# Gathered rows scaled and shifted while they are turned, instead of before they are stored

## The chip, the cores and the metric

The kernel runs on one core of one Trainium2 chip. Its time is the device time of one execution in microseconds (us), given as the median of several executions. The profile is of one further execution of the same program; its rows are in us from the start of its span, and durations in columns called "mean ns" are in nanoseconds.

## The reference

A trunk of two layers over 512 rows of 1024 numbers. Each layer has a mixer (layer 0: retention beside chunk attention; layer 1: stick-breaking attention), an output projection, and a mixture of 16 experts of which a router picks two for each row. What matters here is what stands between the mixer and the experts:

```python
mod = (c_act @ ada_w[layer] + ada_b[layer])[:, None, :]
sh1, sc1, g1, sh2, sc2, g2 = jnp.split(mod, 6, axis=-1)
...
x = x + g1 * mix
h = rms_norm(x, norm2_g[layer]) * (1.0 + sc2) + sh2
x = x + g2 * grouped_moe(h, router_w, router_b, exp_w_gate[layer],
                         exp_w_up[layer], exp_w_down[layer])
...
for e in range(N_EXPERTS):                       # in grouped_moe, t = h
    he = jax.nn.silu(t @ w_gate[e]) * (t @ w_up[e])
    y = y + combine[:, e:e + 1] * (he @ w_down[e]).astype(jnp.float32)
```

So a row h that an expert reads is x times A2 (the gain times 1 + sc2, one number per column), times 1/rms (one number per row), plus B2 (that is sh2, the shift, one number per column).

## The kernel before, in words

**The output projection** (`outproj`) handles the rows in four tiles t of 128. For each tile, TensorE multiplies the mixer's output by the weights in two halves of 512 columns (L539), `add` multiplies by g1 and adds to x on VectorE (L490, L491), ScalarE sums squares (L493), TensorE turns x (L496) and makes partial router logits from it (L500). GpSimd then multiplies the tile by A2 (L544). `rsqrt` (L90 to L102, on VectorE) makes 1/rms for tiles 0 and 1 together and for 2 and 3 together (`RG`). ScalarE multiplies each tile by its 1/rms (L527), and GpSimd issues a DMA that adds it to `hbuf`, a table of 512 rows in the chip's main memory (L528). SyncE has filled that table with B2 before (L465, four writes of 512 KB), from a B2 that was broadcast over 128 partitions by another DMA.

**The gate** runs for tiles 0 and 1, then for 2 and 3: the router's sigmoid on ScalarE (L681), some forty small VectorE operations, and then products on TensorE with one-hot matrices (L742, L743) that make a list of rows for each expert: 32 columns `inv`, 16 of row numbers plus one and 16 of weights. `indices` makes the gather's integer indices `gidx` from them in three operations (L762 to L764), with a number beyond the table for empty places.

**The experts** (`moe`). Four numbers computed from the counts pick one of several written-out variants by a branch (L1311): how many rows an expert may have is fixed for each position of the order, so a position is full (128 rows) or few (64 or 32 rows). For each position GpSimd gathers that expert's rows from `hbuf` by an indirect DMA into one of two buffers X, printed as `x` (L935). They must be turned, so that the 1024 columns lie on partitions: eight transposes of 128 x 128 on TensorE into two PSUM banks for a full expert (`turn`, L950), eight of 64 x 64 or 32 x 32 into one bank for a few one (`turned`, L1069). ScalarE and VectorE copy the result out as a high and a low part (L959, L960), or ScalarE alone as float32 (`fewT`, one buffer, L1070). Then follow the products with gate and up weights (L1008 to L1013 for full experts, three for each pair; L1082 for few ones, in float32, recorded twice each), the activation, a second turn of its result `he` (the same lines), the products with the down weights (L1039, L1082) and a scatter. A few units at the end handle rows beyond the fixed numbers. Weights come in by DMAs of 512 KB which SyncE issues (L121), and 27 of them are on the chip when the experts begin. ScalarE and VectorE split the weights of full experts (L109, L110).

The order of instructions on each engine is set by a scheduler at build time; an engine then runs its list strictly in that order.

## Time and profile before

| | us |
|---|---|
| median of 3 executions | 1280.57 |
| lowest and highest | 1279.33, 1289.4 |
| profiled execution, its time | 1282.25 |
| its span | 1280.4 |
| experts of layer 0: first turn to the end of the experts' products | 366.72 to about 632 |
| experts of layer 1: the same | 992.00 to about 1263 |

The span covers all that the engines do; about 2 us of the execution's time lie outside it. The two stretches of experts are some 40% of the span. Between the last product of the output projection and the first turn, one chain of small steps runs over VectorE, ScalarE, TensorE and GpSimd.

### The profile page before, as it was taken

Reading aid. Unit: us, or ns where it says so; the run is one execution under the profiler, and the core shown is the slowest. Engines: PE = TensorE matmul, PEld = TensorE weight load, DVE = VectorE, ACT = ScalarE, POOL = GpSimd, SP = SyncE. Lnnn points to the kernel's source line nnn. Section 1 sums busy time; section 2 is a strip of 40 time slices with the busy share of each in tenths; the row PEclk is TensorE's granted clock in tenths of the full one; section 3 lists DMA queues with packets and bytes.
Section 4 is the critical chain, followed back from the end, with each engine's and each line's share of the span. In section 5 each row is a group of like instructions: output and inputs, shape, how many; then the busy total and the mean of one; then the engine's idle time right before and its main releaser. Section 6 shows DMA issues by size and latency. Waiting matters only on the chain. (4 is left out here: it accounts for less than half of the span.)

```text
span 1280.4 us, 17584 instructions
## 1 busy us (share of the span) xinstructions
PE 1127.2 (88%) x5992; PEld 763.7 (60%) x5992; DVE 768.5 (60%) x1309; ACT 527.6 (41%) x893; POOL 157.2 (12%) x243
## 2 busy tenths in 40 slices
PE   5999969999759989999679998999984999989894
PEld 3786537778637745575367556756673366656561
DVE  3787679364669744553354789566555367666751
ACT  3325633323236433432144654466431255555530
POOL 2000100010322221112200000000122112211101
PEclk9999969999769989999989989999995899999997
DMA  9986557854669999999783554513458899999982
GB/s 350 363 300 198 157 164 241 291 184 148 190 171 408 362 361 401 384 373 329 261 328 109 181 184 133 200 50 148 163 209 242 318 395 378 377 358 379 352 349 31
DMA packets 96576, 336.79 MB, mean 263 GB/s; under 512 B 13828, under 2 KB 13892, under 8 KB 96340
## 3 DMA queue, kind: packets, MB, share of 16 engines
q1 hardware_dynamic: 85764, 308.59, 65.1%
q0 software_dynamic: 10416, 25.33, 8.4%
q10 hardware_dynamic: 288, 1.57, 0.3%
q8 instruction: 51, 0.84, 0.3%
q14 instruction: 57, 0.47, 0.1%
HBM read 319.13 MB, written 24.81 MB: 269 GB/s over the span
## 5 line engine op out<-in xcount | busy, mean ns | idle before, releaser
L110 DVE TENSOR_TENSOR wl<-w,wh 128x1024 fp32r<-128x1024 f32 x168 | 200.8, 1221 | 83.6 <-ACT wh L109 82.1
L109 ACT CAST wh<-w 128x1024 fp32r<-128x1024 f32 x168 | 172.4, 1050 | 189.4 <-PE mm L280 119.9
L280 PE MATMUL mm<-wh,hT 128*128 128x512 f32 x448 | 145.6, 400 | 2.5 <-DVE Q L577 1.8
L1082 PE MATMUL mo<-w,fewT 128*32 128x256 f32 (+1 forms) x884 | 130.4, 491 | 1.3 <-ACT fewT L1070 1.3
L280 PE MATMUL mm<-hT,wh 128*128 128x512 f32 x384 | 127.2, 404 | 0.0
L168 DVE SCALAR_TENSOR_TENSOR w<-w,cs,w 128x1024 f32<-128x1024 f32 x70 | 89.7, 1281 | 25.7 <-DMA w<-ada_w 25.0
L280 PEld LDWEIGHTS mm<-wh,hT 128*128 128x128 f32 x448 | 84.4, 190 | 22.0 <-issue 1.9
L280 PE MATMUL mm<-wl,hT 128*128 128x512 f32 x224 | 89.4, 399 | 0.0
L280 PEld LDWEIGHTS mm<-hT,wh 128*128 128x128 f32 x384 | 72.0, 191 | 17.0 <-issue 2.8
L1082 PEld LDWEIGHTS mo<-w,fewT 128*32 128x32 f32 (+1 forms) x884 | 41.9, 124 | 64.2 <-issue 49.1
L110 DVE TENSOR_TENSOR wl<-we,wh 128x1024 fp32r<-128x1024 f32 x62 | 73.5, 1220 | 9.8 <-ACT wh L109 9.0
L280 PE MATMUL mm<-hT,wl 128*128 128x512 f32 x192 | 77.3, 404 | 0.0
L109 ACT CAST wh<-we 128x1024 fp32r<-128x1024 f32 x62 | 62.4, 1048 | 20.2 <-PE mo L1012 12.2
L1039 PE MATMUL mo<-wh,fix 128*128 128x512 f32 x224 | 67.0, 406 | 2.4 <-ACT wh L109 2.4
L1082 PE MATMUL mo<-we,fewT 128*64 128x512 f32 (+1 forms) x388 | 67.1, 506 | 0.0
L635 DVE TENSOR_TENSOR_SCAN O<-O,sep 128x1284 f32<-128x1284 f32 x16 | 44.4, 2819 | 23.0 <-ACT O L631 23.0
L935 POOL DMA_INDIRECT x<-hbuf,gidxp x26 | 30.3, 1165 | 193.8 <-PE tr L1069 102.9
L1008 PE MATMUL mo<-wh,fix 128*128 128x512 f32 x112 | 47.0, 420 | 4.9 <-ACT wh L109 4.9
L1009 PE MATMUL mo<-wl,fix 128*128 128x512 f32 x112 | 45.8, 409 | 6.1 <-DVE wl L110 6.1
L1039 PEld LDWEIGHTS mo<-wh,fix 128*128 128x128 f32 x224 | 41.7, 192 | 14.3 <-ACT wh L109 3.3
L280 PEld LDWEIGHTS mm<-wl,hT 128*128 128x128 f32 x224 | 42.5, 190 | 8.8 <-issue 1.0
L959 ACT CAST fix<-tr 128x512 fp32r<-128x512 f32 x42 | 23.8, 587 | 57.7 <-PE tr L950 35.9
(361 smaller groups left out, 2048.4 us busy)
## 6 DMA issues: line engine op xcount, KB each, us to landing
w<-ada_w SPq DMA_DIRECT2D x96, 512.0 KB
w<-w_up SPq DMA_DIRECT2D x80, 512.0 KB
w<-w_down SPq DMA_DIRECT2D x80, 512.0 KB
w<-w_gate SPq DMA_DIRECT2D x79, 512.0 KB
we<-w_gate SPq DMA_DIRECT2D x46, 512.0 KB
we<-w_up SPq DMA_DIRECT2D x44, 512.0 KB
we<-w_down SPq DMA_DIRECT2D x43, 512.0 KB
w<-even_w_in SPq DMA_DIRECT2D x28, 512.0 KB
```

Of the source, the lines that this page charges most:

```text
L109: nc.scalar.copy(h, raw)
L110: nc.vector.tensor_tensor(l, raw, h.bitcast(F32), ALU.subtract)
L168: nc.vector.scalar_tensor_tensor(acc, w, self.cs[:, k:k + 1], acc, ALU.mult, ALU.add)
L280: nc.tensor.matmul(ps[m], x, y, start=(first and i == 0), stop=(last and i == 2))
L635: nc.vector.tensor_tensor_scan(O[:, ::-1], O[:, ::-1], self.sep[:, ::-1], 0.0, ALU.mult, ALU.add)
L935: nc.gpsimd.indirect_dma_start(out=X[0:n], out_offset=None, in_=self.hbuf[0:S, :], in_offset=bass.IndirectOffsetOnAxis(ap=col(c)[0][0:n], ...
L959: nc.scalar.copy(H[:, 0, a:b], pt[:, a:b])
L1008: nc.tensor.matmul(pg, xh, gh[:, s], start=st, stop=False)
L1009: nc.tensor.matmul(pg, xh, gl[:, s], start=False, stop=False)
L1039: nc.tensor.matmul(pd[h], x, y[:, h * 512:(h + 1) * 512], start=(st and i == 0), stop=(sp and i == len(tri) - 1))
L1082: nc.tensor.matmul(ps[r, 0:w], x, ys[i // k][:, (i % k) * w:(i % k + 1) * w], start=st, stop=sp, tile_position=(0, r.start))
```

## The change

Rows go to `hbuf` as x times A2 alone. The fill with B2, its broadcast, the scaling on ScalarE (L527) and the accumulation go; a tile is written by a plain DMA right after the multiplication. Tiles 2 and 3 are multiplied in halves, so that their first halves need not wait for the second, and the last half goes to VectorE; 1/rms is made for tile 2 and tile 3 apart.

1/rms enters the lists as a third group of 16 columns, by the same one-hot products (48 columns in place of 32). For each turn of gathered rows ScalarE makes a 128 x 128 diagonal matrix `dg` from it (`scaled`, one buffer), and TensorE turns the rows by true float32 products with `dg` in place of transposes, so that each row is scaled as it is turned. Ahead of them, one product per PSUM bank (`shift`) puts B2 there: a 40-row matrix holding the high and low parts of B2, by a selecting matrix `sel`. The second turns (of `he`) stay transposes. Indices come from the lists without `indices`, by a table of row numbers that is offset by 1024. The products that reorder the lists for the experts behind the first three (`places`) become three on GpSimd, of 169 columns each, in place of one of 338; the lists of the units at the end get the third group too.

```diff
@@ -38,13 +39,13 @@
-HU = (3,)
+HU = (2, 3)
...
-RG = {1: (0, 1), 3: (2, 3)}
+RG = {1: (0, 1), 2: (2,), 3: (3,)}
@@ -458,11 +459,16 @@
         A2 = self.bcast(self.ov, "ov", mod[l, 4096:5120])
-        B2 = self.bcast(self.ov, "ov", mod[l, 3072:4096])
         ng = self.bcast(u, "u", self.a["n2g"][l])
         nc.vector.scalar_tensor_tensor(A2, A2, 1.0, ng, ALU.add, ALU.mult)
-        for t in range(NT):
-            nc.sync.dma_start(self.hbuf[t * 128:(t + 1) * 128, :], B2)
+        b2 = self.hf.tile([128, 512], F32, tag="hf", name=self.nm("b2"))[0:40, 0:128]
+        nc.gpsimd.memset(b2, 0.0)
+        for o in (0, 32):
+            nc.gpsimd.dma_start(b2[o:o + 8, :], mod[l, 3072:4096].rearrange("(k p) -> k p", k=8))
+        self.b2s = self.rt.tile([40, 128], F32R, tag="b2s", name=self.nm("b2s"))
+        nc.scalar.copy(self.b2s, b2)
+        nc.vector.tensor_tensor(self.b2s[32:40, :], b2[32:40, :], self.b2s[32:40, :].bitcast(F32), ALU.subtract)
         tl = self.sm.tile([1, 1], F32, tag="tl", name=self.nm("tl"))
@@ -483,12 +489,16 @@
+        hs = [*xs[0:2], self.ov.tile([128, 1024], F32, tag="ov", name=self.nm("h")), g1]
         def add(t, ps, half):
...
             nc.vector.tensor_tensor(x[:, s], x[:, s], f, ALU.add)
+            if t in HU and half == 0:
+                nc.gpsimd.tensor_tensor(hs[t][:, s], x[:, s], A2[:, s], ALU.mult)
             j = self.hf.tile([128, 1024], BF, tag="hf", name=self.nm("junk"))[:, 0:512]
@@ -516,20 +526,11 @@
         def rows_done(ts):
             n, a = len(ts), ts[0]
-            r = self.rsqrt(self.sm, ss[:, a:a + n, 0], n, D, f"n{n}", ss[:, a:a + n, 1])
-            def write():
-                for t in ts:
...
-                    nc.scalar.activation(h, h, AF.Copy, scale=r[:, t - a:t - a + 1])
-                    nc.gpsimd.dma_start(self.hbuf[rows, :], h, accum_op=ALU.add)
...
-            return [r[:, i:i + 1] for i in range(n)], write
-        r, hs = [], []
+            r = self.rsqrt(self.sm, ss[:, a:a + n, 0], n, D, f"n{a}", ss[:, a:a + n, 1])
+            return [r[:, i:i + 1] for i in range(n)]
+        r = []
         for t in range(NT):
@@ -540,13 +541,15 @@
             nc.sync.dma_start(dst[rows, :], xs[t])
-            hs.append(g1 if t in HU else xs[t])
-            nc.gpsimd.tensor_tensor(hs[t], xs[t], A2, ALU.mult)
+            if t in HU:
+                c = slice(512, 1024)
+                (nc.vector if t == NT - 1 else nc.gpsimd).tensor_tensor(hs[t][:, c], xs[t][:, c], A2[:, c], ALU.mult)
+            else:
+                nc.gpsimd.tensor_tensor(hs[t], xs[t], A2, ALU.mult)
+            (nc.sync if t == NT - 1 else nc.gpsimd).dma_start(self.hbuf[rows, :], hs[t])
             if t in RG:
-                q, write = rows_done(RG[t])
-                r += q
-                if t < NT - 1:
-                    write()
+                r += rows_done(RG[t])
             for q in LG[t]:
@@ -556,11 +559,10 @@
             self.gate(ts, lp, r, lb)
-            if 3 in ts:
-                write()
         nc.scalar.activation(tl, self.g["pos"][0:1, 3, 0:1], AF.Silu)
+        self.rs = r
         self.yt, self.g2, self.xg = xs[2], xs[3], xs[0:XG]
...
+        return self.gidx, self.g["sl"]
@@ -726,16 +728,18 @@
         nc.vector.tensor_tensor(w, w, rs[:, :, None].to_broadcast([128, n, 2]), ALU.mult)
...
         nc.vector.tensor_tensor(mk, self.io128[:, None, None, 0:NE].to_broadcast([128, n, 2, NE]),
...
         nc.vector.tensor_tensor(R[:, :, :, 0], mk, self.tok1[:, tr, None, None].to_broadcast([128, n, 2, NE]), ALU.mult)
+        for i in range(n):
+            nc.vector.tensor_scalar(R[:, i, :, 2], mk[:, i], r[t0 + i], None, ALU.mult)
         nc.vector.tensor_tensor(R[:, :, :, 1], mk, w[:, :, :, None].to_broadcast([128, n, 2, NE]), ALU.mult)
...
-        pi = self.aux.tile([128, 2, NE], F32, tag="aux", name=self.nm("inv"))
+        pi = self.aux.tile([128, 3, NE], F32, tag="aux", name=self.nm("inv"))
         for t in ts:
@@ -743,26 +747,13 @@
         if t0 == 0:
-            nc.vector.tensor_copy(G["sl"], pi)
+            nc.vector.tensor_scalar(G["sl"][:, 0], pi[:, 0], VOID, None, ALU.add)
+            nc.vector.tensor_copy(G["sl"][:, 1:3], pi[:, 1:3])
         else:
+            self.gidx = self.rt.tile([128, NE], I32, tag="gidx", name=self.nm("gidx"))
+            self.last_dve = nc.vector.tensor_tensor(self.gidx, pi[:, 0], G["sl"][:, 0], ALU.add)
             nc.vector.tensor_tensor(G["sl"], pi, G["sl"], ALU.add)
         self.last_act = nc.scalar.copy(G["pos"][:, tr, :], pp)
-    def gate_idx(self):
-        return self.indices(self.g["sl"], NE, "", self.gt)
-    def indices(self, sl, n, sfx, pool, gidx=None):
-        nc = self.nc
-        tk = sl[:, 0]
-        z = pool.tile([128, n], F32, tag="z", name=self.nm("z"))
-        f1 = pool.tile([128, n], F32, tag="f1", name=self.nm("f1"))
-        if gidx is None:
-            gidx = self.rt.tile([128, n], I32, tag="gidx" + sfx, name=self.nm("gidx"))
-        nc.vector.tensor_scalar(z, tk, 0.5, None, ALU.is_lt)
-        nc.vector.scalar_tensor_tensor(f1, z, 4096.0, tk, ALU.mult, ALU.add)
-        self.last_dve = nc.vector.tensor_scalar(gidx, f1, -1.0, None, ALU.add)
-        return gidx, sl
@@ -806,20 +797,22 @@
         M = NE - NS
...
         gidx, slp = self.placed
...
         nc.vector.tensor_tensor(Pm, pe[:, None, NS:].to_broadcast(sh), self.io128[:, 0:M, None].to_broadcast(sh), ALU.is_equal)
...
         nc.vector.tensor_copy(self.perm, pf)
-        (nc.gpsimd if PP else nc.vector).tensor_tensor(big, Pm[:, None, :, :].to_broadcast(s4),
-                                                       self.g["sl"][:, :, None, NS:].to_broadcast(s4), ALU.mult)
-        nc.vector.tensor_reduce(slp, big, AX.X, ALU.add)
-        self.indices(slp, M, "p", sm, gidx)
+        for i in range(3):
+            nc.gpsimd.tensor_tensor(big[1 + i], Pm, self.g["sl"][:, i, None, NS:].to_broadcast(sh), ALU.mult)
+            nc.vector.tensor_reduce(slp[:, i], big[1 + i], AX.X, ALU.add)
+            if i == 0:
+                nc.vector.tensor_copy(gidx, slp[:, 0])
@@ -941,13 +934,29 @@
-        def turn(src, n, tag, tiles, raw):
+        def scaled(c):
+            dg = m.tile([128, 128], F32, tag="dg", name=self.nm("dg"), bufs=1)
+            nc.scalar.activation(dg, self.ident, AF.Copy, scale=col(c)[2])
+            return dg
+        def shift(pt, ks):
+            nc.tensor.matmul(pt, self.b2s, self.sel[:, ks, None].to_broadcast([40, *pt.shape[1:]]), start=True, stop=False)
+        def turn(src, n, tag, tiles, raw, c=None):
             full = {}
+            dg = None if c is None else scaled(c)
             for g in range(n // 4):
                 pt = self.aux.tile([128, 4, 128], F32, tag="aux", name=self.nm("tr"))
+                if dg is not None:
+                    shift(pt, slice(g * 4, g * 4 + 4))
                 for k in range(4):
-                    nc.tensor.transpose(pt[:, k, :], src[:, (g * 4 + k) * 128:(g * 4 + k + 1) * 128], self.ident)
+                    b = src[:, (g * 4 + k) * 128:(g * 4 + k + 1) * 128]
+                    if dg is None:
+                        nc.tensor.transpose(pt[:, k, :], b, self.ident)
+                    else:
+                        nc.tensor.matmul(pt[:, k, :], b, dg, start=False, stop=(k == 3))
                 r = [k for k in range(4) if g * 4 + k in raw]
@@ -960,8 +969,8 @@
-        def xT(X, mode=BA):
-            return turn(X, 8, "xT", fix[0:2], [2 * kp + i for kp in mode[0] for i in range(2)])
+        def xT(X, c, mode=BA):
+            return turn(X, 8, "xT", fix[0:2], [2 * kp + i for kp in mode[0] for i in range(2)], c)
@@ -1059,18 +1068,24 @@
                 u.he = (X if he is None else he)[u.o, 0:512]
...
                 u.idx = i[0:n] if idx is None else idx[0:n]
-            def turned(u, src, m, dst):
+            def turned(u, src, m, dst, dg=None):
                 pt = self.aux.tile([128, m, u.n], F32, tag="aux", name=self.nm("tr"))
+                if dg is not None:
+                    shift(pt, slice(0, m))
                 for k in range(m):
-                    nc.tensor.transpose(pt[:, k, :], src[:, k * 128:(k + 1) * 128], self.ident[u.o, u.o])
+                    b = src[:, k * 128:(k + 1) * 128]
+                    if dg is None:
+                        nc.tensor.transpose(pt[:, k, :], b, self.ident[u.o, u.o])
+                    else:
+                        nc.tensor.matmul(pt[:, k, :], b, dg[u.o, u.o], start=False, stop=(k == m - 1))
                 nc.scalar.copy(dst, pt)
             def turn(u):
-                u.turned(u.X, 8, u.xt)
+                u.turned(u.X, 8, u.xt, scaled(u.c))
```

TensorE, inside the experts of the variant that layer 0 ran: the turn of the rows of a full expert (`x`, into two PSUM banks `tr`), between products of a few expert (`mo`). Before:

```order
L1013 MATMUL mo_3195<-wh_3226,fix_3020 128x512
L1082 MATMUL mo_3309<-we_2397,fewT_3022 64x512 x2
L950 MATMUL tr_3312<-ident,x_2401 128x128 x4
L950 MATMUL tr_3319<-ident,x_2401 128x128 x4
L1082 MATMUL mo_3309<-we_2398,fewT_3022 64x512 x2
```

After:

```order
L1022 MATMUL mo_3222<-wh_3253,fix_3037 128x512
L1097 MATMUL mo_3336<-we_2404,fewT_3039 64x512 x2
L944 MATMUL tr_3341<-sel,b2s_2383 128x512
L959 MATMUL tr_3341<-dg_3339,x_2408 128x128 x4
L944 MATMUL tr_3349<-sel,b2s_2383 128x512
L959 MATMUL tr_3349<-dg_3339,x_2408 128x128 x4
L1097 MATMUL mo_3336<-we_2405,fewT_3039 64x512 x2
```

The turn stands at the same place, with a shift per bank and products with `dg` in place of transposes.

TensorE, at the start of the experts, right behind the branch (L1311 before, L1326 after). Before:

```order
L1311 COMPARE_AND_BRANCH
L1069 MATMUL tr_3132<-ident,x_2401 128x64 x8
L950 MATMUL tr_3179<-ident,x_2403 128x128 x4
L950 MATMUL tr_3186<-ident,x_2403 128x128 x4
L1082 MATMUL mo_3142<-w_3031,fewT_3022 64x512
```

After:

```order
L1326 COMPARE_AND_BRANCH
L944 MATMUL tr_3151<-sel,b2s_2383 128x512
L944 MATMUL tr_3204<-sel,b2s_2383 128x512
L944 MATMUL tr_3212<-sel,b2s_2383 128x512
L1084 MATMUL tr_3151<-dg_3149,x_2408 128x64 x8
L1097 MATMUL mo_3162<-w_3048,fewT_3039 64x512
```

The shifts of the first two experts come first; the second expert's turn, which stood ahead of the first expert's products (`mo`), stands behind the gate and up products of that expert now.

GpSimd, from the last multiplications by A2 to the first gathers (`x<-hbuf,gidx`). Before:

```order
L544 TENSOR_TENSOR x_2405<-x_2405,bc_2368 128x1024
L544 TENSOR_TENSOR bc_2366<-x_2407,bc_2368 128x1024
L528 DMA hbuf<-x_2405 128x1024
L528 DMA hbuf<-bc_2366 128x1024
L1167 MEMSET he_3109 1x1
L1167 MEMSET fewT_3022 1x1
L935 DMA x_2401<-hbuf,gidx_2995 128x1024
```

After:

```order
L501 TENSOR_TENSOR bc_2372<-x_2414,bc_2374 128x512
L549 TENSOR_TENSOR x_2408<-x_2408,bc_2374 128x1024
L550 DMA hbuf<-x_2408 128x1024
L549 TENSOR_TENSOR x_2410<-x_2410,bc_2374 128x1024
L550 DMA hbuf<-x_2410 128x1024
L547 TENSOR_TENSOR h_2416<-x_2412,bc_2374 128x512
L550 DMA hbuf<-h_2416 128x1024
L1182 MEMSET he_3126 1x1
L1182 MEMSET fewT_3039 1x1
L928 DMA x_2408<-hbuf,gidx_3011 128x1024
```

The last tile's write is no longer in this list (SyncE issues it), and the half tiles `h` and `bc` are multiplied apart.

## Rows read from the trace of the kernel before

**Rows 1.** Stretches: busy PE, PEld, DVE, ACT, POOL; clock, DMA share.

```profile
400.00:420.00 20.00, 20.00 (x146) 15.09 (x145) 17.87 (x20) 13.90 (x17) 5.86 (x5) 1.00 0.99 377
...
1250.00:1280.40 30.40, 13.08 (x64) 4.12 (x59) 3.50 (x5) 0.96 (x2) 4.37 (x3) 0.77 0.22 32
```

**Rows 2.** Waits of TensorE, experts of layer 0.

```profile
PE tr L1069 <- DVE he L1097: 3.8, 4, 1.3
```

**Rows 3.** Waits of TensorE, experts of layer 1.

```profile
PE tr L1069 <- DVE he L1097: 5.1, 4, 1.5
```

**Rows 4.** Waits of SyncE's queue, experts of layer 1.

```profile
SPq L121 <- DMA w<-w_up: 31.9, 28, 3.9
```

**Rows 5.** Timeline of TensorE, a full turn: transposes.

```profile
393.25 1.09 PE L950 MATMUL tr<-ident,x 128*128 128x128 f32 x8
```

**Rows 6.** The same, products with a diagonal, layer 1.

```profile
656.67 1.95 PE L249 MATMUL tr<-dg,x 128*128 128x128 f32 x16
```

**Rows 7.** The same, a few turn of 64 rows: transposes.

```profile
447.45 0.71 PE L1069 MATMUL tr<-ident,x 64*128 64x64 f32 x8
```

**Rows 8.** The same, float32 products of 16 columns.

```profile
930.25 0.96 PE L500 MATMUL plog<-rw,xt 128*128 128x16 f32 x8
...
971.91 1.89 PE L500 MATMUL plog<-rw,xt 128*128 128x16 f32 x8 [0.69 <-ACT xt L498]
```

**Rows 9.** The same, products of 512 columns, layer 1.

```profile
1196.47 0.39 PE L1013 MATMUL mo<-wh,fix 128*128 128x512 f32 x1
1196.69 0.39 PE L1008 MATMUL mo<-wh,fix 128*128 128x512 f32 x1
```

**Rows 10.** All turns of gathered rows of full experts.

```profile
L950 PE MATMUL tr<-ident,x x112: 270/273/447, 369.5 to 1188.0; 128*128 128x128 f32 x112
```

**Rows 11.** The same for few experts.

```profile
L1069 PE MATMUL tr<-ident,x x144: 220/223/338, 366.7 to 1231.6; 64*128 64x64 f32 x96, 32*128 32x32 f32 x48
```

**Rows 12.** VectorE, end of the output projection and gate, layer 0.

```profile
343.74 1.77 DVE L491 TENSOR_TENSOR x<-x,gm 128x512 f32<-128x512 f32 x1
346.31 1.67 DVE L90 SCALAR_TENSOR_TENSOR m<-ss 128x2 f32<-128x2 f32 x1 [0.79 <-ACT junk L493]
...
350.02 0.38 DVE L680 SCALAR_TENSOR_TENSOR lg<-lp,y,lb 128x16 f32<-128x16 f32 x2
351.38 0.19 DVE L682 TENSOR_TENSOR sel<-sc,rb 128x32 f32<-128x32 f32 x1 [0.98 <-ACT sc L681]
...
359.57 0.15 DVE L764 TENSOR_SCALAR gidx<-f 128x16 int32<-128x16 f32 x1
```

**Rows 13.** ScalarE, the same stretch.

```profile
350.08 1.15 ACT L527 ACTIVATE x<-x,y 128x1024 f32<-128x1024 f32 x1 [2.65 <-DVE lp L507]
```

**Rows 14.** GpSimd, the same stretch.

```profile
342.59 2.38 POOL L544 TENSOR_TENSOR x<-x,bc 128x1024 f32<-128x1024 f32 x1 [8.89 <-PE inv L743]
345.60 2.36 POOL L544 TENSOR_TENSOR bc<-x,bc 128x1024 f32<-128x1024 f32 x1 [0.63 <-DMA we<-w_up]
...
361.35 0.09 POOL L1167 MEMSET fewT<- 1x1 f32 x1 [7.77 <-DMA hbuf<-bc]
362.36 1.16 POOL L935 DMA_INDIRECT x<-hbuf,gidx  x1 [0.92 <-DVE qq L850]
```

**Rows 15.** TensorE, start of the experts of layer 0.

```profile
366.72 1.08 PE L1069 MATMUL tr<-ident,x 64*128 64x64 f32 x8 [7.86 <-DMA x<-hbuf,gidx]
369.46 1.94 PE L950 MATMUL tr<-ident,x 128*128 128x128 f32 x8 [1.66 <-DMA x<-hbuf,gidx]
```

**Rows 16.** TensorE, few products at the start of layer 1.

```profile
994.73 9.76 PE L1082 MATMUL mo<-w,fewT 128*64 128x512 f32 x32
```

**Rows 17.** The same number of products late in layer 1.

```profile
1231.73 7.09 PE L1082 MATMUL mo<-we,fewT 128*64 128x512 f32 x32
```

**Rows 18.** VectorE, early in the output projection of layer 1.

```profile
934.03 1.22 DVE L463 SCALAR_TENSOR_TENSOR bc<-bc,bc 128x1024 f32<-128x1024 f32 x1 [4.05 <-DMA bc<-n2g]
935.17 0.68 DVE L491 TENSOR_TENSOR x<-x,gm 128x512 f32<-128x512 f32 x1
```

More of the change, by code (lines that the diff above doesn't have):

```diff
@@ L30 @@
 NL = 2 + NX
+VOID = 1024
 PP = True
@@ L673, in gate @@
                           pos=X([128, 4, 16], "pos"), w=X([128, 4, 2], "w"),
-                          sl=self.rt.tile([128, 2, NE], F32, tag="sl", name=self.nm("sl")))
+                          sl=self.rt.tile([128, 3, NE], F32, tag="sl", name=self.nm("sl")))
         G = self.g
@@ L808, in places @@
         M = NE - NS
-        sh, s4 = [128, M, M], [128, 2, M, M]
-        key, Pm, big, pf = T([128, M], "key"), T(sh, "Pm"), T(s4, "big"), T([1, M], "pf")
+        sh = [128, M, M]
+        key, Pm, pf = T([128, M], "key"), T(sh, "Pm"), T([1, M], "pf")
+        big = [self.xt.tile(sh, F32, tag="big", name=self.nm("big"), bufs=1) for _ in range(4)]
         gidx, slp = self.placed
@@ L868, in overflow @@
             nc.vector.tensor_reduce(v[:, i], tmp, AX.X, ALU.add)
-        px = self.logp.tile([128, 2 * NL], F32, tag="log", name=self.nm("xinv"))
-        R = T([128, 4, 2, 2, NL], "xR")
+        px = self.logp.tile([128, 3 * NL], F32, tag="log", name=self.nm("xinv"))
+        R = T([128, 4, 2, 3, NL], "xR")
         for t in range(NT):
@@ L873, in overflow @@
             for k in range(2):
-                for i, val in ((0, self.tok1[:, t:t + 1]), (1, G["w"][:, t, k:k + 1])):
+                for i, val in ((0, self.tok1[:, t:t + 1]), (1, G["w"][:, t, k:k + 1]), (2, self.rs[t])):
                     nc.vector.tensor_scalar(R[:, t, k, i], self.lists, v[:, 0, t, k:k + 1], val,
                                             ALU.is_equal, ALU.mult)
-                oh = sm.tile([128, 128], F32, tag="oh", name=self.nm("oh"), bufs=2)
+                oh = sm.tile([128, 128], F32, tag="oh", name=self.nm("oh"), bufs=1)
                 nc.vector.tensor_scalar(oh, self.io128, v[:, 1, t, k:k + 1], None, ALU.is_equal)
@@ L880, in overflow @@
                                  stop=(t == 3 and k == 1))
-        nc.vector.tensor_copy(slx, px.rearrange("p (a n) -> p a n", a=2))
-        self.indices(slx, NL, "x", sm, gidx)
+        nc.vector.tensor_copy(slx, px.rearrange("p (a n) -> p a n", a=3))
+        nc.vector.tensor_scalar(gidx, slx[:, 0], VOID, None, ALU.add)
         nc.vector.tensor_copy(low64, gidx[64:128, 1:2])
@@ L1119, in turn @@
             def turn(u):
-                turn(u.X, 8, "xT", u.xt, [])
+                turn(u.X, 8, "xT", u.xt, [], u.c)
             def banks(u):
@@ L1213, in turnX @@
                     return None
-                return xT(Xs[p])
+                return xT(Xs[p], seq[p])
             def turnH(p):
@@ L1376, in body @@
             nc.gpsimd.memset(N.lims[:, i:i + 1], v)
+        N.sel = cst.tile([40, 8], F32R, name="sel")
+        sel = cst.tile([40, 8], F32, name="sel0")
+        nc.gpsimd.memset(sel, 0.0)
+        for o in (0, 32):
+            nc.vector.tensor_copy(sel[o:o + 8, :], N.ident[o:o + 8, o:o + 8])
+        nc.vector.tensor_copy(N.sel, sel)
         N.first = cst.tile([128, 4], F32, name="first")
```

24 lines of the change are left out of this document (10 added, 14 removed).

## The prediction, before any run of the changed kernel

> **What bounds the kernel now.** I read the busy time by stretch first, since the change touches two kinds of stretch: the short one between the output projection and the experts, and the long one of the experts, twice each. In the experts TensorE is busy without a gap over whole stretches at the full clock, 20.00 of 20.00 us, while the DMA engines are as full, at a share of 0.99 [rows 1]. Either could be the bound, so the waits come next. In the experts after their first turn TensorE waits on no DMA of weights; its largest repeated waits are for the activation `he`, 3.8 us in layer 0 and 5.1 in layer 1, in four waits each [rows 2, 3]. SyncE's queue does wait for DMAs, 31.9 us on one tile alone in layer 1 [rows 4], so the transfers run as fast as they can, but they run ahead: in the last 30.40 us the DMA share is 0.22 while TensorE still works for 13.08 us [rows 1]. So **TensorE's list bounds the experts**, with the transfers close behind it, and what lengthens that list lengthens the kernel.
>
> In the short stretch one chain bounds. VectorE adds x for the last tile, then makes 1/rms, then the logits [rows 12]; the router's sigmoid stands on ScalarE behind the scaling L527 [rows 13]; the gate runs to the indices at 359.57 [rows 12]; GpSimd waits 7.77 us until the last rows have landed in `hbuf` and gathers at 362.36 [rows 14]; TensorE waits 7.86 us for these rows and turns them at 366.72, then the second expert's at 369.46 [rows 15]. Layer 1 shows the same.
>
> **What the turns cost.** A full turn is eight transposes in 1.09 us [rows 5]. The change makes it eight float32 products by a diagonal. The kernel does exactly this elsewhere: eight such products (each recorded twice) take 1.95 us [rows 6]. That is 0.86 more. Two shifts are added, each a product of 512 columns; these follow one another at 1196.69 - 1196.47 = 0.22 us [rows 9]. A full turn so costs 0.86 + 0.44 = 1.30 us more. A few turn of 64 rows takes 0.71 us now [rows 7]. Its float32 products have 64 columns or 32. If time went with columns, eight would take 1.95 / 2 = 0.98 or 0.49. But products of only 16 columns take 0.96 us for eight records [rows 8], so 1.92 for sixteen: no cheaper than 128 columns. The narrow row is the nearer one, and I take 1.92. With a shift of 0.22 (64 rows) or half of it (32 rows) the extra is 1.92 - 0.71 + 0.22 = 1.43 or 1.32 us, and by columns 0.49 or about -0.11; for 32 rows I set the transposes at 0.71 as well.
>
> How many: the gathered tile is turned 112 / 8 = 14 times in full, 96 / 8 = 12 times with 64 rows, 48 / 8 = 6 times with 32 [rows 10, 11]; the three units of layer 0 turn one more of each, from another tile. Of these 35 the first two of each layer belong to the start (one full and one few of 64 in layer 0, two few of 64 in layer 1). The rest are 14 full, 10 of 64 rows and 7 of 32: 14 x 1.30 + 10 x 1.43 + 7 x 1.32 = 18.2 + 14.3 + 9.2 = **41.7 us** (by columns 18.2 + 4.9 - 0.8 = 22.3). They stand in TensorE's list where the transposes stood, between products, so they are on the path. What can hide them is TensorE's idle time next to a turn: the waits for `he`, 3.8 + 5.1 = 8.9 us at most. The turn of the next rows stands beside such a wait only at some positions, so I take 4, with 0 and 8.9 as ends.
>
> Here a rule speaks against the change more than the row. The products take 1.95 / 1.09 = 1.8 times the transposes [rows 5, 6]. The Trainium skill (TensorE: Matmul & The Clock Gate, Terms) says of the transpose mode of trn2's matmuls that it is "4× faster for FP32". By that a full turn would go from 1.09 to 4.36 us. The row is of the same operation on the same shape, and decides.
>
> **The diagonals** are 35 small operations on ScalarE, which no row shows; the copy of a 128 x 512 bank is the sort nearest to it and ScalarE is far from full (13.90 of 20.00 us [rows 1]). I take nothing for them; what stands behind them in ScalarE's list are casts of weights, and TensorE's turn waits for them (a rival, below).
>
> **The start of the experts.** Four things move it.
> - The add of x takes 1.77 us and the first step of 1/rms 1.67 us, each beside a GpSimd product of 2.38 or 2.36 us [rows 12, 14]; the same add elsewhere takes 0.68 [rows 18]. The halves and VectorE's share take much of that GpSimd work away. The add can give 1.77 - 0.68 = 1.09. Then the logits wait for partial products on TensorE that take 1.89 us at the half clock [rows 8] and end at about 349.4 in layer 0; 1.09 earlier that is 348.3. The logits, now done at 350.02 + 0.38 = 350.40, come at about 348.9 after two small additions.
> - The sigmoid no longer stands behind L527, which ends at 351.23 with its first tile [rows 13]; `sel`, now at 351.38 [rows 12], comes at about 349.1, 2.3 earlier.
> - The gate loses the three index operations (0.5) and gains two small products for 1/rms (0.4) on VectorE: nothing. So the indices come 2.3 to 2.8 earlier, at about 357.
> - The gather waits for the landing of the accumulation no more, since the last tile's plain write is issued before the gate begins. Now the gather starts 362.36 - 359.72 = 2.64 after the indices; I take 0.6 for that. It starts at about 357.6, **4.8 earlier** (between 2.3, if a write still lands late, and 5.3).
>
> The first rows land 366.72 - 362.36 = 4.36 after that, at 362.0. Their turn is 16 passes at the half clock, at most 2 x 1.89 = 3.8 us by the row of 16 columns [rows 8] in place of 1.08 [rows 15]: 2.7 of the 4.8 go. What is given back: before, the products of the first expert also waited for the second expert's rows and turn (to 369.46 + 1.94 = 371.40 [rows 15]); now that turn stands behind them. The first products so start at 362.0 + 3.8 + 0.7 (copy) = 366.5, 4.8 earlier than 371.3, but the second turn then costs its 1.9 us there. Layer 0 gains about 2.8 at the second expert, layer 1, whose second turn was the shorter one, about 2.4. I take **-5.2** in all, with ends 0 (the longer turn eats it) and 2 x 4.8 = 9.6.
>
> A second rule bears on this place. The granted clock is half when the first products begin: the few products that take 7.09 us at the full clock [rows 17] take 9.76 at the start of layer 1 [rows 16], with only transposes ahead of them. The Trainium skill (TensorE: Matmul & The Clock Gate, Part 4: PE-mode transpose) says that transposes don't count as activity for the clock as products do. By that the new turns would raise the clock sooner and give at most 9.76 - 7.09 = 2.67 us a layer, 5.3 in all, and the sum would be 26 in place of 31. The rows fit it but don't separate it from a rise that merely needs time, and I don't count it.
>
> **The output projection.** Of layer 1, VectorE waits 4.05 us for the last of four broadcasts [rows 18]; one broadcast and the fills of 2 MB go, two tiny DMAs come. A quarter of the wait is 1.0; ends 0 and 4. The accumulations' reading and the fills otherwise run beside other work, and I take nothing for them.
>
> **The sum.** 41.7 - 4 - 5.2 - 1.0 = +31.5 us. Against the profiled 1282.25 that is 1313.8; that execution is 1.7 above the median, so 1280.57 + 31.5 = **1312**. Low end: 22.3 - 8.9 - 9.6 - 4 = -0.2, the time of before. High end: 41.7 - 0 = 1322.
>
> **Rivals.**
> - *The transfers bound the experts, not TensorE.* For it: a DMA share of 1 and SyncE waiting for DMAs. Then the longer turns cost nothing as long as they fit into slack that the trace doesn't show as waits, and the earlier start counts in full: -9.6 - 1.0 and up to -4 more, 1266 to 1270. It decides if TensorE's gapless stretches are only modelled ends. Against: TensorE shows no wait for weights, and its products follow at their own pace [rows 9].
> - *Few turns go by columns and hide well.* Then the low end holds: 1280 to 1290, no measurable change. Against: the 16-column row.
> - *The diagonal comes late.* There is one `dg`, made in ScalarE's list among casts of weights (the scaling L527, of the same 1024 columns, takes 1.15 [rows 13]). If every turn waits for one, 31 x 1.15 = 36 us come on top; for half of them 18: 1330 to 1348. It decides wherever ScalarE reaches the diagonal after TensorE would need it. Against: ScalarE has idle time.
> - *The products take four times the transposes.* 14 x (3 x 1.09 + 0.44) + 17 x (3 x 0.71 + 0.2) = 52 + 40 = 92 in place of 41.7: 1362. This is the factor of the page named above, which the Trainium skill gives; the row of 1.95 us is against it.
>
> **How the numbers follow.** A measurement of this kernel can tell about 1%, 12.8 us, from no change. Forecast (1292 to 1325) 0.62; transfers bound 0.14; columns and hiding 0.14; late diagonals 0.08; factor four 0.02. Faster by over 1% (below 1267.8) holds in the better part of the first rival, 0.09; within 1% in its rest, in the second, and not quite in the forecast, 0.2; slower 0.71. The range reaches from 1266 to 1330: it leaves out the end of the first rival and most of the last two.
>
> **What would show it.** In the profile after: eight products by `dg` near 1.95 us for full and few turns alike; two shifts of 0.22; expert stretches of TensorE longer by about 20 us each; the DMA share there below 1; the first gather 4 to 5 us earlier; `sel` 2.3 earlier. Wrong would be few turns near 1 us, waits of TensorE for `dg`, or a last load that ends as close to TensorE's end as now with an unchanged length of the experts, which would mean that the transfers set it.

## The result: slower by 3.0%, in the range and a little above the forecast

The changed kernel takes 1318.41 us (median of 4 executions, 1315.46 to 1319.23) beside 1280.27 for the kernel before: a ratio of 1.0302, 95% interval 1.0265 to 1.0339. The forecast was 1312. On a second chip the same pair gave 1316.45 and 1279.83, 1.0295 (1.0251 to 1.0339).

The start of the experts came earlier than forecast, and the experts became longer than forecast. The timeline of VectorE after, at the end of the output projection and in the gate of layer 0 (start us, us, what):

```profile
342.16 0.68 DVE L499 TENSOR_TENSOR x<-x,gm 128x512 f32<-128x512 f32 x1
...
343.63 0.16 DVE L91 SCALAR_TENSOR_TENSOR m<-ss 128x1 f32<-128x1 f32 x1
...
345.66 0.23 DVE L682 SCALAR_TENSOR_TENSOR lg<-lp,y,lb 128x16 f32<-128x16 f32 x1
346.19 0.19 DVE L684 TENSOR_TENSOR sel<-sc,rb 128x32 f32<-128x32 f32 x1 [0.30 <-ACT sc L683]
...
354.19 0.17 DVE L754 TENSOR_TENSOR gidx<-inv,sl 128x16 int32<-128x16 f32 x1 [0.37 <-PE inv L747]
```

Against [rows 12] the add takes 0.68 us in place of 1.77 and the first step of 1/rms 0.16 in place of 1.67; `sel` comes 5.2 us earlier and the indices 5.4. GpSimd after, the same stretch:

```profile
347.83 0.09 POOL L1182 MEMSET fewT<- 1x1 f32 x1 [4.05 <-DMA hbuf<-bc]
354.66 1.11 POOL L928 DMA_INDIRECT x<-hbuf,gidx  x1 [6.74 <-DVE sl L755]
```

The rows have landed in `hbuf` by 347.8, and the gather waits for the indices alone: it starts 354.66 - 354.36 = 0.3 us after them, 7.7 earlier than in [rows 14]. TensorE after, from there on:

```profile
359.06 3.64 PE L1084 MATMUL tr<-dg,x 64*128 64x64 f32 x16 [1.33 <-DMA x<-hbuf,gidx]
363.43 9.18 PE L1097 MATMUL mo<-w,fewT 128*64 128x512 f32 x32 [0.72 <-ACT fewT L1085]
372.54 2.05 PE L959 MATMUL tr<-dg,x 128*128 128x128 f32 x16
374.37 0.50 PE L1017 MATMUL mo<-wh,fix 128*128 128x512 f32 x1
```

The first turn takes 3.64 us at the half clock (1.08 in [rows 15]), the first expert's products start at 363.43 (371.33 before), and the second turn stands behind them. The second expert starts at 374.37, 6.0 us earlier than before:

```profile
380.41 0.50 PE L1008 MATMUL mo<-wh,fix 128*128 128x512 f32 x1
```

How early this is differs from one execution to the next. In a second profile of the same changed kernel (the second chip's) the first products start at 359.69.

Then the gain is lost. A full turn and a turn of 32 rows in the experts of layer 0 after, and one of 64 rows:

```profile
387.23 0.48 PE L944 MATMUL tr<-sel,b2s 40*128 40x512 f32 x1
387.64 1.16 PE L959 MATMUL tr<-dg,x 128*128 128x128 f32 x8
388.73 0.48 PE L944 MATMUL tr<-sel,b2s 40*128 40x512 f32 x1
389.14 1.16 PE L959 MATMUL tr<-dg,x 128*128 128x128 f32 x8
390.23 2.80 PE L1097 MATMUL mo<-we,fewT 128*64 128x512 f32 x12
...
440.84 0.37 PE L944 MATMUL tr<-sel,b2s 40*128 40x256 f32 x1
441.14 1.97 PE L1084 MATMUL tr<-dg,x 32*128 32x32 f32 x16
443.04 1.50 PE L1097 MATMUL mo<-w,fewT 128*32 128x256 f32 x24
...
596.50 0.48 PE L944 MATMUL tr<-sel,b2s 40*128 40x512 f32 x1
596.82 1.89 PE L1084 MATMUL tr<-dg,x 64*128 64x64 f32 x16
598.64 3.37 PE L1097 MATMUL mo<-w,fewT 128*32 128x256 f32 x32
```

From its first instruction to the next product, the full turn holds TensorE for 390.23 - 387.23 = 3.00 us, the one of 32 rows for 2.20, the one of 64 rows for 2.14. In the kernel before the full turn at 393.25 [rows 5] held it for 1.02, since the next product follows at 394.27:

```profile
394.27 1.08 PE L1082 MATMUL mo<-we,fewT 128*64 128x512 f32 x4
```

To see where the whole difference lies I cut both profiles at the same instructions and, in windows of 2 us, split each stretch of experts into idle time of TensorE, time lost to the half clock (busy time x (1 - granted clock)), and the rest, which is what its list takes at the full clock. The stretches go from the first expert's products to the last 56 (layer 0) or 20 (layer 1) of the last few expert:

| us | before | after | difference |
|---|---|---|---|
| layer 0, up to the first expert's products | 371.3 | 363.4 | -7.9 |
| experts of layer 0 | 257.1 | 288.9 | +31.9 |
| of that: list / idle / half clock | 239.5 / 11.5 / 6.0 | 271.0 / 5.9 / 12.0 | +31.5 / -5.6 / +6.0 |
| from there to layer 1's first products | 366.4 | 360.8 | -5.5 |
| experts of layer 1 | 262.7 | 281.0 | +18.2 |
| of that: list / idle / half clock | 240.3 / 15.0 / 7.5 | 266.6 / 6.5 / 7.9 | +26.3 / -8.5 / +0.4 |

The waits of TensorE in the experts of layer 1 (in us, times, longest), those for split weights before and then all that are over 0.5 us after:

```profile
PE mo L1009 <- DVE wl L110: 5.2, 4, 1.8
PE mo L1008 <- ACT wh L109: 3.2, 2, 1.6
```

```profile
PE tr L1082 <- DVE he L1112: 3.6, 3, 1.5
PE mo L1017 <- ACT wh L110: 1.6, 1, 1.6
PE mo L1018 <- DVE wl L111: 0.6, 1, 0.6
```

Before, `he` cost 5.1 there [rows 3], and the waits for split weights, which I had not counted, 8.4; they went to 2.2. A longer list seems to give ScalarE and VectorE time to split weights: in the profiles of all the experiments below that keep the variant, idle time in the two stretches is 23 to 27 us where the list takes some 480, 12 to 13 where it takes 520 to 540, and 7 where it takes 546.

### The profile page after: what moved, and what is told of

The parts are those of the page before. It is cut to its first block, busy times and chain, and to the rows that moved or that the text cites. A ratio compares the mean times of both kernels' runs of the same rounds, so it can differ in the third digit from the quotient of the medians.

```text
span 1316.8 us, 18263 instructions
## 1 busy us (share of the span) xinstructions
PE 1194.6 (91%) x6322; PEld 819.1 (62%) x6322; DVE 775.5 (59%) x1340; ACT 531.7 (40%) x922; POOL 153.7 (12%) x252
## 5 line engine op out<-in xcount | busy, mean ns | idle before, releaser
L1048 PE MATMUL mo<-wh,fix 128*128 128x512 f32 x224 | 71.1, 425 | 2.4 <-ACT wh L110 2.4
L1085 ACT COPY fewT<-tr 128x256 f32<-128x256 f32 (+2 forms) x40 | 16.9, 423 | 78.7 <-PE tr L1084 37.2
L1017 PE MATMUL mo<-wh,fix 128*128 128x512 f32 x112 | 47.0, 420 | 1.6 <-ACT wh L110 1.6
L1124 DVE TENSOR_TENSOR x<-mo,x 64x512 f32<-64x512 f32 (+1 forms) x48 | 26.6, 554 | 36.5 <-PE mo L1097 35.5
```

Of the source, the lines that this page charges most:

```text
L1017: nc.tensor.matmul(pg, xh, gh[:, s], start=st, stop=False)
L1048: nc.tensor.matmul(pd[h], x, y[:, h * 512:(h + 1) * 512], start=(st and i == 0), stop=(sp and i == len(tri) - 1))
L1085: nc.scalar.copy(dst, pt)
L1124: nc.vector.tensor_tensor(u.y[:, s], pd[r, 0:w], self.g2[r, s], ALU.mult)
```

## The experiments

Four kernels first, on one chip with the kernel before (1278.86 there).

**Plain turns.** In `turn` and `turned` of the changed kernel (neither 1/rms nor B2 reaches the experts):

```diff
-            dg = None if c is None else scaled(c)
+            dg = None
...
-                u.turned(u.X, 8, u.xt, scaled(u.c))
+                u.turned(u.X, 8, u.xt)
```

> The changed kernel with its gathered rows turned by plain transposes: no diagonal, no shift. Each expert then reads x times A2 without 1/rms and without B2, which is left out of the computation; all the rest of the change stays (plain writes, the split 1/rms, the shorter index path, the third group in the lists). Theory (TensorE's list pays for the turns, the earlier start is kept): the time of before less what the start gained in the profile after, 6.0 us in layer 0 and 6.7 in layer 1, so 1280.3 - 12.7 = about 1267.5, and no more than 1272. Rival (the transfers bound the experts, so that an earlier start is given back while weights arrive): 1276 to 1281. Rival (the extra time comes from elsewhere in the change than the turns): above 1290.

Measured: 1270.57 us, ratio 0.9938 (0.9913 to 0.9964). Taking the turns back alone turns 3% slower into 0.6% faster, so the turns, with their diagonals and shifts, make the change slower, and the rest of it gains. The gain against this chip's 1278.86 is 8.3 us where the theory had 12.7. In its profile (an execution of 1276.58 us) the first expert starts as early as after the change (363.01), and the list of the experts is 242.3 and 240.2 us, near that of before; half clock and idle time in the two layers are 45 us where before they were 40. So some of the start was given back, to the clock, though not by waiting for transfers of weights, of which no wait of TensorE's products is listed.

**No shift.** The products by `dg` stay, B2 is left out:

```diff
-                if dg is not None:
-                    shift(pt, slice(g * 4, g * 4 + 4))
...
-                        nc.tensor.matmul(pt[:, k, :], b, dg, start=False, stop=(k == 3))
+                        nc.tensor.matmul(pt[:, k, :], b, dg, start=True, stop=True)
```

(and the same in `turned`).

> The changed kernel without the shift products: rows are turned and scaled by the diagonal, B2 is left out of the computation. Theory (a shift costs TensorE its own time and a change of the kind of product on both sides, about 0.2 us each): a full turn goes from 3.00 us to about 1.8, a few one from 2.14 or 2.20 to about 1.85, so 15 x 1.2 + 13 x 0.3 + 7 x 0.3 = 24 us at most, of which some 5 come back as waits for casts and activations: 1295 to 1300. Rival (a shift costs its columns, 0.22 us, and no more): 15 x 0.44 + 13 x 0.22 + 7 x 0.11 = 10 us, about 1308. Rival (the diagonals on ScalarE are what delays, not the products): not below 1312.

Measured: 1286.56 us, ratio 1.0058 (1.0030 to 1.0085), 31 us below the changed kernel's 1.030 and so beyond even the theory's 24. One or two shifts per turn cost about twice what eight float32 products in place of transposes did (1286.6 - 1270.6 = 16). The rival by which the diagonals on ScalarE delay is out, since this kernel makes them too. Its full turn:

```profile
385.88 2.05 PE L957 MATMUL tr<-dg,x 128*128 128x128 f32 x16
387.86 2.79 PE L1093 MATMUL mo<-we,fewT 128*64 128x512 f32 x12
```

Eight products hold TensorE for 1.98 us here, twice the transposes' 1.02. The list of the experts is 263.9 and 255.9 us, 7.1 and 10.7 less than after, where the turns' times give (3.00 - 1.98) x 6 + 0.3 x 11 = 9.4 and (3.00 - 1.98) x 8 + 0.3 x 6 = 10.0. The rest of the 28 us between the two profiles is half clock (7.3 us in layer 0 in place of 12.0) and, some 5 us, what lies outside the experts. The shifts ahead of the first turn don't explain these 5: behind them TensorE still waits 1.33 us for the rows (the row at 359.06), and from layer 0's experts to layer 1's first products the changed kernel's second profile takes 356.8 us with its shifts, this one 357.1 without them and the changed kernel's first 360.8.

**Shifts first.** The complete change, with both banks' shifts ahead of the eight products:

```diff
+            pts = [self.aux.tile([128, 4, 128], F32, tag="aux", name=self.nm("tr")) for _ in range(n // 4)]
+            if dg is not None:
+                for g, pt in enumerate(pts):
+                    shift(pt, slice(g * 4, g * 4 + 4))
-            for g in range(n // 4):
-                pt = self.aux.tile([128, 4, 128], F32, tag="aux", name=self.nm("tr"))
-                if dg is not None:
-                    shift(pt, slice(g * 4, g * 4 + 4))
+            for g, pt in enumerate(pts):
```

> The changed kernel, complete, with both shifts of a full turn ahead of its eight products, so that the kind of product changes twice in a full turn in place of four times. Theory (each change of kind costs about 0.2 us): 15 full turns x 0.4 = 6 us less, about 1312. Rival (a shift costs its columns alone and the order is indifferent): 1318, within 2 us.

Measured: 1309.02 us, ratio 1.0239 (1.0199 to 1.0280), some 8 us less than the change: the theory, a little more than it. The two intervals overlap, so the times alone are weak; the row shows it:

```profile
386.84 0.70 PE L944 MATMUL tr<-sel,b2s 40*128 40x512 f32 x2
387.46 2.05 PE L960 MATMUL tr<-dg,x 128*128 128x128 f32 x16
389.44 2.79 PE L1098 MATMUL mo<-we,fewT 128*64 128x512 f32 x12
```

The same 18 records hold TensorE for 389.44 - 386.84 = 2.60 us in place of 3.00. The list became 2.0 us (layer 0) and 2.6 (layer 1) shorter, 4.6 where 14 x 0.40 gives 5.6. Of the rest of the gain 4.5 lie between the layers (356.3 us in place of 360.8), which the changed kernel's second profile has as well, so they are not the order's.

**Scale before the store, shift at the copy.** A complete kernel. ScalarE multiplies the rows by 1/rms before the plain write, the last tile behind the router's sigmoid; turns are transposes; VectorE adds B2 as a turned bank is copied; the third group is gone:

```diff
+        def write(ts):
+            for t in ts:
+                nc.scalar.activation(hs[t], hs[t], AF.Copy, scale=r[t])
+                (nc.sync if t == NT - 1 else nc.gpsimd).dma_start(self.hbuf[t * 128:(t + 1) * 128, :], hs[t])
...
-        nc.scalar.activation(sc, lg, AF.Sigmoid)
+        sig = nc.scalar.activation(sc, lg, AF.Sigmoid)
+        if then:
+            with self.tc.issue_after(sig.ins):
+                then()
...
+                if c is not None:
+                    nc.vector.tensor_tensor(pt, pt, self.B2[l][:, g * 4:g * 4 + 4, None].to_broadcast([128, 4, 128]), ALU.add)
...
-                nc.scalar.copy(dst, pt)
+                if b2 is None:
+                    nc.scalar.copy(dst, pt)
+                else:
+                    nc.vector.tensor_tensor(dst, pt, b2[:, :, None].to_broadcast([128, m, u.n]), ALU.add)
```

> A complete kernel that keeps what the change did at the start and takes the turns back: ScalarE multiplies the rows by 1/rms before they are stored, the last tile only after the router's sigmoid, plain writes as in the change, turns by transposes, and B2 is added by VectorE when a turned bank is copied out (in place of ScalarE's copy for few experts, one more operation of about 0.7 us per bank for full ones). The third group of the lists is gone. Theory (TensorE's list bounds, VectorE has room): the start is as early as after the change and the turns cost TensorE what they did before: 1266 to 1272, faster than both kernels. Rival (the additional VectorE step lies between turn and products and TensorE waits for it in every turn): 31 x 0.7 = 22 us on top, about 1290. Rival (the last tile's rows land too late and the gather waits for them): 2 to 4 us a layer on top of the theory, 1272 to 1278.

Measured: 1269.77 us, ratio 0.9932 (0.9908 to 0.9957): faster than both kernels, as the theory had it. The rival of a wait in every turn is out by the time, that of late rows by the rows of ScalarE and GpSimd:

```profile
345.34 0.23 ACT L682 ACTIVATE sc<-lg 128x32 f32<-128x32 f32 x1 [1.63 <-DVE lg L681]
345.48 1.13 ACT L528 ACTIVATE bc<-bc,y 128x1024 f32<-128x1024 f32 x1
```

```profile
353.60 1.11 POOL L928 DMA_INDIRECT x<-hbuf,gidx  x1 [2.93 <-DVE kf L775]
```

The scaling now follows the sigmoid, and the gather waits for VectorE, not for rows to land. So the early start needs neither the diagonal nor the shift on TensorE. It is not all kept: 9.1 us of the 12.7. In this profile the first products of layer 0 start 8.5 us earlier than before, but the last products of its experts only 2.7 earlier (625.66 in place of 628.38), with 3.4 us more of list and 3.0 more of half clock between them, and among the last products TensorE waits 0.55 us for weights, the only such wait listed there.

Two more, on another chip (before: 1280.77).

**Whole multiplication.** The tiles are multiplied by A2 in one piece on GpSimd again:

```diff
-            if t in HU and half == 0:
-                nc.gpsimd.tensor_tensor(hs[t][:, s], x[:, s], A2[:, s], ALU.mult)
...
-            if t in HU:
-                c = slice(512, 1024)
-                (nc.vector if t == NT - 1 else nc.gpsimd).tensor_tensor(hs[t][:, c], xs[t][:, c], A2[:, c], ALU.mult)
-            else:
-                nc.gpsimd.tensor_tensor(hs[t], xs[t], A2, ALU.mult)
+            nc.gpsimd.tensor_tensor(hs[t], xs[t], A2, ALU.mult)
```

> The changed kernel, complete, with each tile multiplied by A2 in one piece on GpSimd once the tile is done, as in the kernel before, in place of halves and of VectorE's share for the last tile. Theory (beside GpSimd's long product VectorE's add and the first steps of 1/rms are slow): the add of the last half tile goes back from 0.68 to about 1.8 us and the first step of 1/rms from 0.16 to up to 1.7, so the gate comes 1 to 2.6 us later in each layer, and the last tile's write with it: 2 to 5 us in all, a ratio to the kernel before higher by 0.002 to 0.004 than the changed kernel's 1.030. Rival (the start was gained by the split 1/rms and the sigmoid's place alone): no difference from 1.030.

Measured: 1319.96 us, ratio 1.0320 (1.0279 to 1.0360), which doesn't tell the two apart by itself; the rows do. GpSimd and VectorE in the gate of layer 0:

```profile
341.43 2.39 POOL L543 TENSOR_TENSOR bc<-x,bc 128x1024 f32<-128x1024 f32 x1 [5.65 <-DVE x L499]
```

```profile
340.66 0.69 DVE L499 TENSOR_TENSOR x<-x,gm 128x512 f32<-128x512 f32 x1
...
342.14 1.69 DVE L91 SCALAR_TENSOR_TENSOR m<-ss 128x1 f32<-128x1 f32 x1 [0.60 <-ACT junk L501]
...
346.08 0.19 DVE L678 TENSOR_TENSOR sel<-sc,rb 128x32 f32<-128x32 f32 x1 [0.30 <-ACT sc L677]
```

The add keeps its 0.69, since the product starts only behind it, but the first step of 1/rms is slow again beside that product, 1.69 us, and ends when the product ends (342.14 + 1.69 = 343.83, 341.43 + 2.39 = 343.82). From the add's start to `sel` 346.08 - 340.66 = 5.42 us go by, in layer 1 as well; after the change it is 346.19 - 342.16 = 4.03. So the halves and VectorE's share gain 1.4 us a layer, the lower part of what the theory said. This stretch took 7.64 us before [rows 12]. Of the other 2.2, half is the add itself (1.77 to 0.69): it stood beside the product of the tile before it, from 342.59 on [rows 14], which starts at 332.54 here. The rest lies between the first step of 1/rms and `sel`, where the sigmoid's place is free.

**Shift twice.** Each shift is issued twice in a row (B2 is added twice):

```diff
-            nc.tensor.matmul(pt, self.b2s, self.sel[:, ks, None].to_broadcast([40, *pt.shape[1:]]), start=True, stop=False)
+            for i in range(2):
+                nc.tensor.matmul(pt, self.b2s, self.sel[:, ks, None].to_broadcast([40, *pt.shape[1:]]), start=(i == 0), stop=False)
```

> The changed kernel with every shift product issued twice in a row, which adds B2 twice; all else is the same. Theory (a second shift behind the first changes no kind of product and so costs its columns): 0.22 us for 512 columns and 0.11 for 256, 30 x 0.22 + 13 x 0.22 + 7 x 0.11 = 10 us, a ratio to the kernel before of about 1.038. Rival (a shift costs 0.4 to 0.6 us in itself, whatever stands beside it): 43 x 0.5 + 7 x 0.4 = 24 us, a ratio of about 1.049.

Measured: 1302.17 us, ratio 1.0176 (1.0137 to 1.0215): *faster* than with one shift, against both. The same cut of its profile: the list of the experts grew by 4.3 and 3.8 us, which is the theory's price, while half clock went from 12.0 and 7.9 us to 8.1 and 2.0 and idle time from 5.9 and 6.5 to 3.2 and 3.6. In all that is 7 us for the experts. The other 6 of the 13.5 us between the two profiles lie outside them, where profiles of one kernel differ as much: layer 0's first products come 2.8 us earlier here, at 360.62, and 3.7 earlier in the changed kernel's second profile.

Three last ones, on one chip (before: 1279.83), to see whether this is the kernel's or a chance: the changed kernel and the one with two shifts again, and one with three (`range(3)`).

> The changed kernel itself, beside the other two on one chip. Theory: 1.030 as on the first chip, within 0.004. Rival (the first value was that chip's): nearer to the kernel with the shift twice, 1.018.

Measured: 1316.45 us, ratio 1.0295 (1.0251 to 1.0339).

> The kernel with each shift twice once more (B2 is added twice). Theory (its higher clock belongs to the order of its instructions, not to one chip): 1.018 within 0.004, and in the profile again a smaller sum of half clock and idle time in the experts than the changed kernel. Rival (a chance of that run): 1.035 or more, the changed kernel's ratio and the columns' price.

Measured: 1302.52 us, ratio 1.0180 (1.0133 to 1.0226). It is the kernel's. In the experts of the two layers half clock cost 15.2 + 7.9 us in the changed kernel's second profile, and 3.7 + 1.5 with two shifts. Here the whole gain is in the experts: 292.0 and 281.0 us became 282.4 and 275.5.

> Each shift product issued three times (B2 is added three times). With each shift twice the kernel came out faster than with one, against both theories of that run; in the profiles the time of TensorE's list in the experts, with half clock and idle time taken off, still grew by 4.3 and 3.8 us, while half clock and idle time fell by 15 in the two layers. Theory (a further product costs its columns, 8 to 10 us, and what it gave before was clock dips, of which few are left): slower than with two, a ratio to the kernel before of 1.021 to 1.027. Rival (each further product keeps the clock up and gives more than it takes): below 1.015. Rival (the fast result with two was the state of one chip or run): near the changed kernel's own ratio and above, 1.035.

Measured: 1422.10 us, ratio 1.1113 (1.1059 to 1.1167), which answers nothing. With the rows of layer 0 so far off, layer 1 routes otherwise and runs another variant: 352 records of full products with the diagonal in place of 224. (The kernels with no shift, plain turns and two shifts kept the variant: their counts of turns are those of before.) Layer 0 alone can be compared: its experts took 284.1 us there, with 4.4 of half clock, beside 288.9 and 292.0 with one shift and 286.6 and 282.4 with two. A third shift gives no more there.

## Why the prediction was right, and where its terms were off

**The bound.** That TensorE's list bounds the experts was right: plain turns brought the list, and with it the time, back. The rival of the transfers is out: longer turns cost the kernel 3%, no wait of TensorE's products for a transfer of weights is listed after, the share of the DMA engines in the experts fell from 0.98 and 0.96 to 0.90 and 0.91, and about two thirds of the gained start (8.3 and 9.1 of 12.7 us) stayed in both kernels that kept the turns short.

**The turns, 41.7 us.** This is the term that was too small. The list grew by 31.5 + 26.3 = 57.8 us; of this the second expert's turn, which I had put in the start, is 1.9 in layer 0 and about as much in layer 1, so that some 54 stand against 41.7. By kind: a full turn costs 3.00 - 1.02 = 1.98 us more, not 1.30; 64 rows about 1.5 (1.43 forecast), 32 rows about 1.6 (1.32). 14 x 1.98 + 10 x 1.5 + 7 x 1.6 = 54. That narrow float32 products are no cheaper held: 1.89 and 1.97 us for 64 and 32 columns, 2.05 for 128. The shift was mis-sized. I took its 0.22 us from a row in which products of one kind follow one another [rows 9]. Between the shift and the float32 products behind it 387.64 - 387.23 = 0.41 us go by, and eight records split off by a shift hold TensorE for 1.09 (388.73 - 387.64), where sixteen in a row take 1.98. A second shift behind the first adds only 0.62 - 0.41 = 0.21 (387.46 - 386.84 = 0.62 for two), and the list of the kernel with two shifts grew by 8.1 us, near the columns' price of 14 x 0.44 + 10 x 0.22 + 7 x 0.11 = 9.1 for the turns in these stretches. So what was missing is some 0.2 us at the step from a shift to the float32 products and 0.1 for each group of eight that a shift splits off, and issuing the shifts together saves 0.40 of it per full turn. That it is the change of kind that costs this is argued: the shift also has 40 partitions in place of 128 and other operands, and these were not tried apart.

**Hidden, 4 us.** Idle time fell by 14.1. I looked only at waits for `he` [rows 2, 3] and called them the largest that repeat, which in layer 1 they were not: those for `wl`, 5.2 us in four, were as large. By the lists of waits some 9 of the 14 were waits for split weights (8.4 us to 2.2 in layer 1, 4.9 to 2.4 in layer 0), 2.8 one wait for the rows of an extra unit in layer 0, and `he` gave only 1.8.

**The start, 5.2 us, and the output projection, 1.0.** Together 7.9 - 1.9 in layer 0 and about 5.5 - 1.9 in layer 1 at the second expert, so 9.6 against 6.2. From the last tile's add to the first products, which leaves out what differs from profile to profile ahead of it, the change gains 6.3 and 5.3 us (6.6 and 5.7 in the second profile), less 1.9 each. I had the gather 4.8 us earlier and it came 7.7 earlier. In this profile the last tile itself was done 1.6 earlier (its add at 342.16 in place of 343.74 [rows 12]); in the second one 5.0. From the add to `sel` 3.6 us were gained where I had 2.3: I let only the add count, because the partial products would end late at the half clock (1.89 us [rows 8]). They ran at the full clock (1.00 granted, 0.50 before), so that the first step of 1/rms counted too, 1.67 to 0.16 us:

```profile
344.35 1.06 PE L510 MATMUL plog<-rw,xt 128*128 128x16 f32 x8 [0.70 <-ACT xt L508]
```

The steps that I named were right: the sigmoid freed, GpSimd's long product out of the way, the landing no longer waited for (2.3 us, where I had 2.0).

**The clock, not counted.** Half clock cost 6.4 us more in the experts of this profile, and 9.6 more in the second. The rule of the Trainium skill (TensorE: Matmul & The Clock Gate, Part 4: PE-mode transpose), by which products in the turns would raise the clock sooner, would have given up to 5.3 us. The first products of layer 0 take 9.18 us behind a turn of products and 9.14 behind one of transposes in the kernel before, and 8.58 with plain turns. Over the two layers of all these kernels they take 8.56 to 9.96 us behind products and 8.29 to 9.76 behind transposes, so nothing of it shows here.

**The factor four** of the Trainium skill (TensorE: Matmul & The Clock Gate, Terms) is out: eight products hold TensorE for 1.98 us, eight transposes for 1.02.

**Late diagonals** are out as well: no wait of TensorE's products for `dg` is listed after (the loads of their weights show two waits of 0.4 us in layer 0), and the kernel without shifts makes the same 35 diagonals, of 0.40 us each, and is 31 us faster.

The errors of the terms, +12 for the turns, -10 for hiding, -3 for the start and +6 for the clock, mostly cancel. The mechanism was right, but that the forecast came within 7 us of the time is in part luck.

## What to carry to other kernels

Where TensorE's list is the bound, work that is cheap elsewhere should not be folded into its instructions: here 1/rms belongs on ScalarE ahead of the store and the shift on VectorE at the copy, and some 9 of the 12.7 us that the change gained at the start are kept. A product's price should be read from a row in which the same neighbours stand beside it. And an experiment that alters values can send a kernel down another branch; count its instructions before using its time.

## What the hardware showed that was not expected

TensorE's granted clock fell to half with no idle time before it. The stretches after, around a turn of 32 rows that ended at 408.23 (first the length and the busy time of TensorE, then the other engines; the third number from the end is the granted clock):

```profile
406.00:408.00 2.00, 2.00 (x17) 1.85 (x17) 1.89 (x2) 1.02 (x2) 0.00 (x0) 1.00 1.04 424
408.00:410.00 2.00, 2.00 (x8) 1.64 (x8) 0.50 (x2) 1.60 (x3) 0.94 (x1) 0.66 1.02 408
410.00:412.00 2.00, 2.00 (x6) 1.54 (x6) 1.25 (x2) 1.04 (x1) 0.00 (x0) 0.50 0.94 373
412.00:414.00 2.00, 2.00 (x10) 1.65 (x9) 1.17 (x1) 1.05 (x1) 0.00 (x0) 0.99 0.22 70
```

TensorE is busy for all of the 2.00 us in each, and the clock goes from 1.00 to 0.50 and back: some 1.7 us lost.

The traces of all these kernels show what such falls share. In the experts (layer 1 of the kernel with three shifts left out) there are 21 falls with no idle time, or at most 0.05 us, in the 6 us before them, two in the changed kernel's first profile and four in its second. Each of them comes around the end of a turn of 32 rows by products, 1.97 us as in the row at 441.14 above, and none at a turn of 64 or 128 rows. The three kernels that turn these rows by transposes (the one before, the one with plain turns, the one that scales before the store) have no such fall. All other falls, theirs too, come within some 3 us of a wait of 0.9 to 2.8 us. Not every turn of 32 rows brings a fall, and what about it does so is open: I have not tried it apart.

In the experts the changed kernel has seven falls in its first profile and nine in its second, five of each behind waits. With two shifts per turn there are three and one, all at turns of 32 rows and none behind a wait; idle time is 6.8 us there in place of 12.4. So a kernel that does more was faster by 1.2%, in two runs: its list is 8.1 us longer, but 5.6 us of idle time and 10 to 18 of half clock are gone. Why the falls behind waits are gone is not shown; one wait of 1.5 us for `he` is still listed, with no fall behind it.
